# A finished head group's skip, gate and squares one tile per half unit, and the squares written over the gate

## The chip, the cores and the metric

The kernel runs on one core of a Trainium2 chip. A core has a matrix engine (TensorE, PE in the profile, with its weight loads as PEld), a vector engine (VectorE, DVE), a scalar engine (ScalarE, ACT), a general engine (GpSimd, POOL) and a queue engine that issues most DMAs (SyncE, SP). The metric is device time of one launch in microseconds.

## The reference

One step of a two-layer decoder over 512 prompt tokens and 8 x 4 sample tokens, 544 columns in all, of width 1024. Layer A is a Mamba-2 mixer: a projection to a gate `z` (2048), to `x|B|C` (3072) and to `dt`; a causal convolution of width 4 with SiLU on `x|B|C`; a chunked recurrence over 32 heads in 4 groups; then

```python
y, s_final = ssd_scan(xs * dt[..., None], dt * a, bm, cm, ssm_init.astype(jnp.float32))
y = y + xs * d_skip.astype(jnp.float32)[:, None]
y = rmsnorm(y.reshape(b, l, SSM_INNER) * jax.nn.silu(z.astype(jnp.float32)), g_gate)
return y.astype(h.dtype) @ w_out, new_conv, s_final
```

Three things of this are done for each finished head group, and the change is about them: the skip (`y + xs * d_skip`), the gate (times SiLU of `z`), and the squares that the norm needs. Layer B is a dilated window attention on a shared K/V; a last RMSNorm ends the step. Layer B, the K/V projection and the norms behind the layers are not touched.

## The kernel before

Features lie on the 128 partitions, tokens on the free axis, so one tile of a feature block is 128x544. A head group has 512 inner features, four such tiles, held together in one "slab" of 128x4x544. The pool `slab` has 13 of them; the halves of the normalized input (`xh`, `xl`, four slabs), `BT` and `CT`, the recurrence's output `v`, its input `xs`, the gate `uz` and later the split outputs `vh`, `vl` all come from it. A slab is free again when the last instruction that reads it is done.

Matrix products are done in three passes on a split of float32 into a high and a low part, 24 matmuls for one half of the tokens: `pa` for columns 0 to 255, `pb` for 256 to 543. Three PSUM banks (tag `pj`) serve all projections, five (tag `ss`) the recurrence.

*The units.* The recurrence is cut into 24 units, six per group: four chunks of 128 prompt tokens and, after the second and the fourth, two quads of four sample rows each (`ssm_chunk`, L602; `ssm_quad`, L663). Each unit is a generator with a first part (load, decay, transposes) and a second part (state update and output, written into `v`); a quad has a third, its last state update, whose store (L746, on ScalarE's DMA queue) frees the buffer for the next quad's load of states (L685, on SyncE's). A quad's states sit in two buffers.

*The filler.* Between these parts the loop draws steps from a filler, one matmul per step: the projections of `x|B|C` and `z`, tile by tile, in the order of `IN_ORDER` (L46 to L51). `PACE` (L55) says how many steps a unit gets: 57, 62, 64 and 44 for the four groups, half of them between the unit's own first part and the second part of the unit before, and half before that unit's third part. A tile of `x`, `B` or `C` ends in `conv`: ScalarE copies the two PSUM halves into `cb` (L331, L336, L337), makes the first product `co` (L527), VectorE adds three more (L529), ScalarE takes the tanh (L531), and VectorE writes the result (L532, L533). GpSimd writes the edges of `cb` (L329, L330) and saves the last rows (L523, L524). A tile of `z` ends in `z_part` (L562): a tanh into `zth`, then VectorE writes the gate into `uz`. A weight tile is split by ScalarE (L199) and VectorE (L200).

*The "t" buffers.* `cb`, `co`, `zth` and `sq` share one tag with four buffers of up to 571 columns:

```python
    def tt(name, cols=T):
        return wk.tile([128, cols], F32, name=name, tag="t", bufs=4)
```

*The finish of a group.* At units 6, 12, 18 and 24 the loop calls `gate_skip` for the group that has just ended. It issues four skips on VectorE (L584), and for every tile whose gate is done already `gate_mul_a`: the product with `uz` (L592; GpSimd, for the last group VectorE), the square on ScalarE into a "t" buffer `sq` (L597; the first of all goes straight into `ssq`, L594), and the sum into `ssq` on GpSimd (L598). Tiles whose gate comes later are multiplied at the end of their `z_tile`.

*What sets the order.* The program is written for a scheduler that puts each engine's instructions in order beforehand, by priority (the written order, but for parts marked as urgent) and by when it expects their inputs and buffers. On the chip every engine then keeps that order; a waiting instruction holds up what stands behind it on its engine.

Of the kernel before, what the change touches and what calls it, by code (L numbers as in the profile page):

```python
# [14 lines left out]
AF = mybir.ActivationFunctionType  # L15
ALU = mybir.AluOpType
# [108 lines left out]
def tile_yoco_step(  # L125
# [6 lines left out]
    nc = tc.nc  # L132
# [21 lines left out]
    def half(name, dt=F32, shape=(128, 4, T)):  # L154
        return slab.tile(list(shape), dt, name=name, tag="s")

    def pj(name, cols=512):
        return psum.tile([128, cols], F32, name=name, tag="pj", bufs=3)
# [61 lines left out]
    def proj_steps(p, ws, act_h, act_l, c0, c1, k0=0, k1=None, order=None):  # L220
        n = len(ws) * 8
        o = p[:, 0:c1 - c0]
        order = order or range(n)
        for i in range(k0, n if k1 is None else k1):
            k = order[i]
            hi, lo = ws[k // 8]
            ah, al = act_h[k // 4][:, k % 4, c0:c1], act_l[k // 4][:, k % 4, c0:c1]
            mm(o, hi[:, k % 8, :], ah, start=i == 0, stop=False)
            yield
            mm(o, hi[:, k % 8, :], al, start=False, stop=False)  # L230
            yield
            mm(o, lo[:, k % 8, :], ah, start=False, stop=i == n - 1)
            yield
# [63 lines left out]
    def tt(name, cols=T):  # L297
        return wk.tile([128, cols], F32, name=name, tag="t", bufs=4)
# [18 lines left out]
    dsk = ac.tile([128, 16], F32, name="dsk")  # L317
# [67 lines left out]
    for i in range(2):  # L385
        sq, xa = sqx[i][:, :, 0:HA], x_t[i][:, :, 0:HA]
# [157 lines left out]
    v_t = [None] * 4  # L544
    xs_t, uz_t = {}, {}
    v_done, z_done = set(), {}
    ssq = ac.tile([128, T], F32, name="ssq")
# [14 lines left out]
    def z_part(g, i, th, p, c0, c1):  # L562
        p = p[:, 0:c1 - c0]
        nc.scalar.activation(th[:, c0:c1], p, AF.Tanh, scale=0.5)
        nc.vector.scalar_tensor_tensor(uz_t[g][:, i, c0:c1], th[:, c0:c1], 1.0, p, op0=ALU.add, op1=ALU.mult)

    def z_tile(zi, w):
        g, i = zi // 4, zi % 4
        if i == 0:
            uz_t[g] = half("uz")  # L570
        th = tt("zth")
        for c0, c1 in ((0, HA), (HA, T)):
            p = pj("pa" if c0 == 0 else "pb")
            yield from proj_steps(p, [w], x_h, x_l, c0, c1)
            z_part(g, i, th, p, c0, c1)
        z_done[g] = i + 1
        if g in v_done:
            gate_mul_a(g, i)

    def gate_skip(g):  # L580
        v, xs = v_t[g], xs_t[g]
        for i in range(4):
            vi = v[:, i, :]
            nc.vector.scalar_tensor_tensor(vi, xs[:, i, :], dsk[:, 4 * g + i:4 * g + i + 1], vi, op0=ALU.mult, op1=ALU.add)  # L584
        v_done.add(g)
        for i in range(z_done.get(g, 0)):
            gate_mul_a(g, i)

    def gate_mul_a(g, i):
        vi, uz = v_t[g][:, i, :], uz_t[g][:, i, :]  # L590
        last = g == 3
        (nc.vector if last else nc.gpsimd).tensor_tensor(vi, vi, uz, op=ALU.mult)  # L592
        if g == 0 and i == 0:
            nc.scalar.activation(ssq, vi, AF.Square)  # L594
            return
        sq = tt("sq")
        nc.scalar.activation(sq, vi, AF.Square)  # L597
        nc.gpsimd.tensor_tensor(ssq, ssq, sq, op=ALU.add)  # L598

    grp = {}  # L600

# [163 lines left out]
    def filler_a():  # L765
        nxt = load_w(w_in[5])
        for i, (kind, t) in enumerate(IN_ORDER):
            if i < 5:
                continue
            w = nxt  # L770
            if i + 1 < len(IN_ORDER):
                nxt = load_w(w_in[i + 1])
            else:
                out_first.append(load_w(w_out[0, :, 0:8, :]))
            yield from (conv_tile if kind == "x" else z_tile)(t, w)
            if kind == "x" and t == 3:
                yield from tok_transposes()
            if kind == "z" and t in (13, 14):
                for j in range(4):
                    v_split(t - 13, j)  # L780

    def run(n):
        for _ in range(n):
            if next(fill, 0) == 0:
                return
# [22 lines left out]
    for u in range(len(units) + 1):  # L808
        pace = PACE[min(u, len(units) - 1) // 6]
        if u < len(units):  # L810
            live.append(units[u][0](*units[u][1]))
            next(live[u])
        run(pace // 2)
        if u:
            next(live[u - 1], 0)
            run(pace - pace // 2)
            next(live[u - 1], 0)
            if u == len(units):
                run(10000)
            if u % 6 == 0:  # L820
                gate_skip(u // 6 - 1)
        else:
            run(pace - pace // 2)
    run(10000)
# [711 lines left out]
    for u in range(len(units) + LA + 2):  # L1536
        i = u - LA
# [111 lines left out]
```

## Time and profile before

| | |
|---|---|
| median of 3 runs | 942.71 us (940.88 to 947.96) |
| the profiled execution | 942.13 us |
| its span | 940.4 us |
| TensorE busy / its mean granted clock | 917.3 us (98%) / 0.991 |
| VectorE, ScalarE, GpSimd busy | 682.7, 479.3 and 203.3 us |
| layer A's recurrence, from its first to its last unit | about 80 to 361 us of the span |
| skips of groups 0 to 3 | from 153.8, 230.1, 305.6 and 361.8 us |

All rows are of one profiled execution; times in them are in microseconds from the start of the span, durations in a group's row are means in nanoseconds. L592 means line 592 of the kernel before. In a list of waits, a row says who waited, for whom, for how long in total, how many times, and the longest. In the chain of waits, a row has its start, its length, and what ran or was waited for. In a table by stretches, a row has the stretch, its length, the busy time of PE, PEld, DVE, ACT and POOL with the number of instructions, then TensorE's granted clock as a share of full speed, the busy share of the DMA engines, and GB/s. In a row of an engine's order, the brackets hold the idle time before it and what ended that.

### The profile page before, as it was taken

What the parts mean: (1) busy time and instruction counts of PE and PEld (TensorE: products, weight loads), DVE (VectorE), ACT (ScalarE), POOL (GpSimd) and SP (SyncE); (2) the same over time, 40 slices, a digit from 0 to 9 for tenths busy, and PEclk for the clock granted to TensorE, in tenths of its full rate; (3) what the DMA queues carried; (4) which work ended last, traced back from release to release, by engine and by line L of the source; (5) the groups of instructions that cost most, each with busy time, mean ns of one, the idle gap of its engine ahead of it and who ended that gap; (6) DMA issues with size and microseconds to landing.
All of it is one profiled execution on the core that took longest, in us unless ns stands there. A gap on an engine that the chain in (4) does not pass through costs nothing.

```text
span 940.4 us, 21836 instructions
## 1 busy us (share of the span) xinstructions
PE 917.3 (98%) x8659; PEld 846.0 (90%) x8659; DVE 682.7 (73%) x1421; ACT 479.3 (51%) x1071; POOL 203.3 (22%) x297
## 2 busy tenths in 40 slices
PE   7999999899899999999999999999999999999996
PEld 5999888789798889999999999988888888888996
DVE  6688988997998889644489336876677766778632
ACT  5557754645555654422255213555555555557642
POOL 2232644723826642111101000000000000000021
PEclk9999999899999999999999999999999999999999
DMA  7252255264454543536277555757767767775411
GB/s 260 89 141 94 101 196 180 93 202 133 165 169 153 182 161 110 157 113 220 89 253 231 185 189 184 268 182 267 245 202 260 266 213 254 267 257 184 155 48 48
DMA packets 75951, 168.49 MB, mean 179 GB/s; under 512 B 19463, under 2 KB 37209, under 8 KB 75337
## 3 DMA queue, kind: packets, MB, share of 16 engines
q1 hardware_dynamic: 71608, 154.63, 50.2%
q10 hardware_dynamic: 3168, 9.72, 2.6%
q0 software_dynamic: 1072, 2.74, 1.1%
q8 instruction: 68, 1.11, 0.5%
q14 instruction: 35, 0.28, 0.1%
HBM read 141.14 MB, written 25.93 MB: 178 GB/s over the span
## 4 chain that ended last, share of the span: by engine, by line
PE 91%; DVE 4%; DMA 2%; ACT 1%; POOL 1%; issue 0%; DVEq 0%; ACTq 0%; SPq 0%
PE pa L143 36%; PE pb L143 31%; PE sp L143 3%; PE so L143 3%; PE pv L143 2%; PE s L143 2%; PE yd L143 2%; PE csp L143 1%; PE yo L143 1%; PE xp L146 1%; PE ptp L146 1%; PE w L146 1%; PE yos L143 1%; PE up L143 1%; POOL v L592 1%; DMA kc<-ck 1%
## 5 line engine op out<-in xcount | busy, mean ns | idle before, releaser
L199 ACT ACTIVATE whi<-wraw 128x1024 fp32r<-128x1024 f32 x72 | 76.1, 1057 | 95.8 <-PE pb L143 63.3
L200 DVE TENSOR_TENSOR wlo<-wraw,whi 128x1024 fp32r<-128x1024 f32 x71 | 89.2, 1256 | 47.0 <-ACT whi L199 46.6
L143 PE MATMUL pa<-bq,whi 128*128 128x272 f32 x512 | 103.1, 296 | 0.0
L143 PE MATMUL pa<-xh,whi 128*128 128x256 f32 (+1 forms) x320 | 93.1, 294 | 3.3 <-ACT xh L365 3.3
L143 PE MATMUL pb<-xh,whi 128*128 128x288 f32 (+1 forms) x304 | 91.0, 301 | 3.9 <-ACT cb L331 3.9
L143 PE MATMUL pb<-xl,whi 128*128 128x288 f32 (+1 forms) x304 | 91.8, 304 | 0.9 <-DVE xl L368 0.8
L143 PE MATMUL pa<-xl,whi 128*128 128x256 f32 (+1 forms) x320 | 90.8, 287 | 1.1 <-DVE xl L368 1.1
L143 PE MATMUL pb<-xh,wlo 128*128 128x288 f32 (+1 forms) x304 | 88.1, 301 | 0.0
L143 PE MATMUL pa<-xh,wlo 128*128 128x256 f32 (+1 forms) x320 | 85.0, 283 | 0.0
L143 PEld LDWEIGHTS pa<-bq,whi 128*128 128x128 f32 x512 | 81.3, 189 | 0.9
L143 PE MATMUL pb<-bq,whi 128*128 128x272 f32 x384 | 77.1, 295 | 0.5 <-DVE kv L1114 0.5
L143 PE MATMUL pa<-bq,wlo 128*128 128x272 f32 x256 | 74.2, 290 | 0.0
L529 DVE SCALAR_TENSOR_TENSOR co<-cb,cvp,co 128x568 f32<-128x568 f32 x72 | 66.3, 921 | 1.1
L143 PEld LDWEIGHTS pa<-xh,whi 128*128 128x128 f32 x320 | 60.9, 190 | 6.2 <-ACT xh L365 3.7
L143 PEld LDWEIGHTS pb<-xl,whi 128*128 128x128 f32 x304 | 58.3, 192 | 6.5 <-issue 4.4
L143 PEld LDWEIGHTS pa<-xl,whi 128*128 128x128 f32 x320 | 60.8, 190 | 3.5 <-DVE xl L368 1.6
L143 PEld LDWEIGHTS pb<-xh,whi 128*128 128x128 f32 x304 | 58.5, 192 | 5.0 <-ACT cb L331 4.1
L143 PEld LDWEIGHTS pb<-bq,whi 128*128 128x128 f32 x384 | 60.8, 189 | 1.6 <-DVE kv L1114 0.8
L1350 POOL COPY lse<-mxs 128x1 f32<-128x1 f32 x16 | 4.6, 287 | 266.9 <-DVE mxs L1348 266.9
L143 PEld LDWEIGHTS pa<-xh,wlo 128*128 128x128 f32 x320 | 58.1, 189 | 1.3 <-issue 0.9
L143 PEld LDWEIGHTS pb<-xh,wlo 128*128 128x128 f32 x304 | 57.2, 192 | 2.2 <-issue 2.2
L1173 ACT ACTIVATE whi<-wraw 128x512 fp32r<-128x512 f32 x64 | 40.1, 627 | 36.7 <-PE pa L143 17.0
(389 smaller groups left out, 2771.0 us busy)
## 6 DMA issues: line engine op xcount, KB each, us to landing
wraw<-w_in SPq DMA_DIRECT2D x40, 512.0 KB
kc<-ck SPq DMA_DIRECT2D x32, 640.0 KB
vc<-cv SPq DMA_DIRECT2D x32, 640.0 KB
wraw<-wb SPq DMA_DIRECT2D x32, 512.0 KB
s<-s SPq DMA_DIRECT2D x16, 512.0 KB
m<-aed SPq DMA_DIRECT2D x16, 512.0 KB
ssmS<-s ACTq DMA_DIRECT2D x16, 512.0 KB
wraw<-w_out SPq DMA_DIRECT2D x16, 512.0 KB
```

The source lines that it names most:

```text
L143: pin(nc.tensor.matmul(*a, **k))
L146: pin(nc.tensor.transpose(*a))
L199: a = nc.scalar.activation(hi, raw, AF.Copy)
L200: b = lo_eng.tensor_tensor(lo, raw, f32(hi), op=ALU.subtract)
L529: nc.vector.scalar_tensor_tensor(o, cb[:, k:k + n], cvp[:, ti, k:k + 1], o, op0=ALU.mult, op1=ALU.add)
L592: (nc.vector if last else nc.gpsimd).tensor_tensor(vi, vi, uz, op=ALU.mult)
L1173: nc.scalar.activation(hi, src[p][j], AF.Copy)
L1350: nc.gpsimd.tensor_copy(lse[:, i16:i16 + 1], mx[:, 2:3])
```

## The change

A finished group's four tiles go into a list `skips`. The loop takes one tile from it at the start of a unit and one in the middle, after the second part of the unit before, so a group's finish is spread over the next two units. The tile's product, square and sum follow its skip at once if its gate is done; otherwise they follow at the end of its `z_tile`, as before, for which the set `v_done` now holds pairs of group and tile. After the last unit the list is emptied before the rest of the filler, where before the filler ran to its end first. The square goes into the tile's own gate `uz`, which the product has just read, and no longer takes a "t" buffer.

```diff
-        if g in v_done:
+        if (g, i) in v_done:
             gate_mul_a(g, i)
 
-    def gate_skip(g):
-        v, xs = v_t[g], xs_t[g]
-        for i in range(4):
-            vi = v[:, i, :]
-            nc.vector.scalar_tensor_tensor(vi, xs[:, i, :], dsk[:, 4 * g + i:4 * g + i + 1], vi, op0=ALU.mult, op1=ALU.add)
-        v_done.add(g)
-        for i in range(z_done.get(g, 0)):
+    skips = []
+
+    def skip_one():
+        if not skips:
+            return
+        g, i = skips.pop(0)
+        vi = v_t[g][:, i, :]
+        nc.vector.scalar_tensor_tensor(vi, xs_t[g][:, i, :], dsk[:, 4 * g + i:4 * g + i + 1], vi, op0=ALU.mult, op1=ALU.add)
+        v_done.add((g, i))
+        if i < z_done.get(g, 0):
             gate_mul_a(g, i)
...
-        sq = tt("sq")
-        nc.scalar.activation(sq, vi, AF.Square)
-        nc.gpsimd.tensor_tensor(ssq, ssq, sq, op=ALU.add)
+        nc.scalar.activation(uz, vi, AF.Square)
+        nc.gpsimd.tensor_tensor(ssq, ssq, uz, op=ALU.add)
...
+        skip_one()
         run(pace // 2)
         if u:
             next(live[u - 1], 0)
+            skip_one()
             run(pace - pace // 2)
             next(live[u - 1], 0)
+            if u and u % 6 == 0:
+                skips += [(u // 6 - 1, i) for i in range(4)]
             if u == len(units):
+                while skips:
+                    skip_one()
                 run(10000)
-            if u % 6 == 0:
-                gate_skip(u // 6 - 1)
         else:
             run(pace - pace // 2)
```

## The prediction

> **What bounds the kernel now.** I read the page's busy times first, then the list of who waited for whom, for the matrix engine alone, from 40 to 420 us (the stage that the change touches), then the chain of waits and the order of the other engines around each wait found.
>
> ```profile
> PE 917.3 (98%) x8659; PEld 846.0 (90%) x8659; DVE 682.7 (73%) x1421; ACT 479.3 (51%) x1071; POOL 203.3 (22%) x297
> ```
> ```profile
> PE pb L143 <- ACT cb L331: 3.9, 1, 3.9
> PE yos L143 <- DMA s<-s: 2.5, 1, 2.5
> ```
>
> TensorE is the bound, and in the touched stage it waits just twice. So the change can win only what these two waits cost, and can lose wherever it makes a third. A table by stretches (us, busy PE, PEld, DVE, ACT, POOL, then the granted clock) gives each wait and what follows it:
>
> ```profile
> 163.83:167.77 3.94, 0.01 (x1) 0.00 (x1) 3.94 (x4) 1.56 (x4) 3.86 (x3) 0.80 0.89 356
> 167.77:173.00 5.23, 5.23 (x23) 5.17 (x23) 5.12 (x7) 3.05 (x9) 4.67 (x8) 0.50 0.00 0
> 244.02:246.55 2.53, 0.00 (x0) 0.00 (x1) 2.50 (x6) 0.64 (x2) 2.36 (x8) 1.00 0.92 303
> 248.00:252.00 4.00, 4.00 (x22) 4.00 (x21) 3.30 (x6) 4.00 (x10) 4.00 (x4) 0.57 0.13 52
> ```
>
> The first wait costs 3.94 us, and then 5.23 us run at clock 0.50, half of which is lost: 2.6. Together 6.5. The second costs 2.53 and then 4.00 x (1 - 0.57) = 1.7, together 4.2. The prize is 10.8 us (6.55 + 4.25 unrounded), no more. A practical rule of the Trainium skill (TensorE: Matmul & The Clock Gate, section Why this matters for your kernels) asks for no idle gaps above about 3 us between bursts; by it the second gap would lose no clock, and the prize would be 9.1. The 0.57 row speaks against it, and I go by the row.
>
> **The first wait: who holds it.** The chain of waits, then ScalarE's own order there:
>
> ```profile
> 161.46 1.80 DVE v L584
> 163.26 0.07 issue
> 163.33 2.24 POOL v L592
> 165.58 1.75 POOL ssq L598
> 167.32 0.02 issue
> 167.34 0.38 ACT cb L331
> 167.73 0.04 issue
> 167.77 0.61 PE pb L143
> ```
> ```profile
> 165.61 0.66 ACT L597 ACTIVATE sq<-v 128x544 f32<-128x544 f32 x1 [2.25 <-POOL v L592]
> 166.17 0.57 ACT L650 COPY st<-csp 128x512 f32<-128x512 f32 x1
> 167.34 0.37 ACT L331 COPY cb<-pa 128x256 f32<-128x256 f32 x1 [0.60 <-POOL ssq L598]
> ```
>
> This is group 0's finish: skip (L584), gate (L592), square (L597), sum (L598). TensorE's next projection needs a PSUM bank that the copy into `cb` frees. That copy lacks a buffer of the four tagged "t", because squares sit in them until GpSimd has summed them; and it also stands on ScalarE behind the last square, which had stood there 2.25 us for GpSimd's product. The change takes away both holds: the square goes over the gate `uz` and takes no "t" buffer, and the four pieces come one per half unit, so at most one or two of the four are still ahead of this copy. I count 6.5 us gained. What is late next is VectorE, below.
>
> **The second wait.** It is another part of the same finish, of group 1:
>
> ```profile
> 230.75 0.49 PE L143 MATMUL up<-xr,btr 32*128 32x512 f32 x1
> ```
> ```profile
> 230.13 5.08 DVE L584 SCALAR_TENSOR_TENSOR v<-xs,dsk,v 128x544 f32<-128x544 f32 x4
> 235.13 1.21 DVE L200 TENSOR_TENSOR wlo<-wraw,whi 128x1024 fp32r<-128x1024 f32 x1
> 236.26 0.80 DVE L529 SCALAR_TENSOR_TENSOR co<-cb,cvp,co 128x568 f32<-128x568 f32 x1
> 236.99 0.68 DVE L744 TENSOR_TENSOR s<-up,s 128x512 f32<-128x512 f32 x1
> ```
> ```profile
> 238.37 4.51 DMA ssmS<-s
> 242.89 0.02 SPq L685
> 242.91 0.03 issue
> 242.94 3.57 DMA s<-s
> 246.51 0.04 issue
> 246.55 1.05 PE yos L143 x4
> ```
>
> The last state update of quad 1 is ready on TensorE at 230.75 + 0.49 = 231.2, but VectorE adds it at 236.99, behind four skips in one piece (5.08). Its store then leaves at 238.37, the load into the same buffer at 242.94, and TensorE wants it at 244.02. With no skip ahead, the update can go about 5.1 us earlier. The store follows the update by 238.37 - 236.99 - 0.68 = 0.7 (ScalarE's queue, held by the same copy into `cb`), so it leaves near 233, and the load lands near 241.4 instead of 246.5, 2.6 us before it is wanted. I count 4.2 gained. Even if two skips stay ahead (half of 5.08), the 2.53 is just gone.
>
> **What the moved steps cost.** Per tile, one VectorE skip, one GpSimd product (VectorE for group 3), one ScalarE square, one GpSimd sum; no DMA. Their grouped rows:
>
> ```profile
> L584 DVE SCALAR_TENSOR_TENSOR v<-xs,dsk,v x16: 772/778/1884, 153.8 to 363.8; 128x544 f32<-128x544 f32 x16
> ```
> ```profile
> L598 POOL TENSOR_TENSOR ssq<-ssq,sq 128x544 f32<-128x544 f32 x15 | 23.7, 1581 | 28.4 <-ACT sq L597 28.0
> L592 POOL TENSOR_TENSOR v<-v,uz 128x544 f32<-128x544 f32 x12 | 21.6, 1805 | 31.1 <-DVE v L584 16.1 <-DVE uz L565 15.0
> ```
>
> Counts and shapes stay, so nothing is saved or added in work. A tile costs GpSimd 1.8 + 1.6 = 3.4 us, and there are four per boundary, 13.6. They move past the next group's first chunk and quad: on GpSimd past the state decays and the small copies into the next `cb`; on ScalarE a square waits for its product with the next copies behind it; on SyncE nothing moves. The square waits for the same product as before, so that wait is not new. Two slabs live longer: `xs` by about one and a half units, `uz` until the sum rather than the product. By my count of live slabs the pool of 13 is just full at groups 1 and 2 (four halves of x, BT and CT, three or four `v`, two `xs`, one or two `uz`) and not over, so I take zero; a first write delayed by one square and sum, 0.66 + 1.6 = 2.3 us, is the other end, beside TensorE's queued matmuls.
>
> The term that I can't read off is VectorE's slack. Its busy time (third) in the stretches after each finish:
>
> ```profile
> 150.00:206.00 56.00, 52.06 (x406) 46.52 (x405) 54.38 (x79) 31.16 (x65) 30.79 (x41) 0.94 0.43 145
> 206.00:230.00 24.00, 24.00 (x205) 21.61 (x204) 17.92 (x36) 13.23 (x32) 8.62 (x16) 1.00 0.48 158
> 230.00:280.00 50.00, 47.47 (x369) 41.73 (x369) 47.61 (x70) 29.38 (x62) 27.04 (x37) 0.97 0.48 160
> 280.00:361.00 81.00, 81.00 (x675) 71.03 (x675) 70.60 (x119) 45.39 (x97) 42.11 (x42) 1.00 0.48 165
> ```
>
> Without the first wait TensorE would pass the first stretch in 56.0 - 6.5 = 49.5 us, with 54.4 of VectorE work beside it: VectorE falls 4.9 us further behind. It has 24.0 - 17.9 = 6.1 us free in the next stretch to recover. In the third, 47.6 against 50.0 - 4.2 = 45.8 leaves 1.8. If the buffers bear no lag, 6.7 us of the prize come back; if they bear all, 0. VectorE ran 97% busy through the first stretch and TensorE waited only where squares held the buffers, so I am nearer to 0 and take 1.5.
>
> **Sum.** The profiled execution took 942.13 us (span 940.4 and 1.7 around it), 0.6 below the median of 942.71. 942.1 - 10.8 + 1.5 = 932.8; I say 933.
>
> **The rivals.**
> *One gap stays.* ScalarE's order is fixed beforehand; a square or a tanh that waits for a late VectorE result still holds the copy into `cb`. For it: 2.25 us of such waiting in the row of 165.61. Against: only one piece at a time now. With the first gap kept, 942.1 - 4.2 = 937.9; with the second kept, 942.1 - 6.5 = 935.6.
>
> *The order hardly moves.* The scheduler places instructions by priority and readiness, so the written place isn't the placed one:
>
> ```profile
> 158.88 0.77 DVE L584 SCALAR_TENSOR_TENSOR v<-xs,dsk,v 128x544 f32<-128x544 f32 x1
> 159.58 1.88 DVE L529 SCALAR_TENSOR_TENSOR co<-cb,cvp,co 128x568 f32<-128x568 f32 x1
> 161.39 1.87 DVE L584 SCALAR_TENSOR_TENSOR v<-xs,dsk,v 128x544 f32<-128x544 f32 x1
> ```
>
> Here skips written in one piece are already split by other work. Then just the freed buffers count: the copy into `cb` gains its 0.60 wait, the store about 0.7; 942.1 - 1.3 = 940.8.
>
> *Slower: VectorE becomes the bound.* A skip takes 0.77 alone and 1.87 beside GpSimd's product, 1.1 more; a convolution step at 159.58 shows the same. If the 8 GpSimd operations of a boundary, now strewn among convolution steps, each lengthened one such step more than before, VectorE would gain 8 x 1.1 = 8.8 us of work per boundary at the low end, and 8 x 1.8 = 14.4 if each blocked for a whole product. Group 0: lag 4.9 + 8.8 to 14.4, less the 6.1 of slack, is 7.6 to 13.2 us of waiting, with 2.6 of slow clock after it; group 1, lag 1.8 and the same additions, has 81.0 - 70.6 = 10.4 us of slack behind it, and gives 0 to 7.5 (5.8 and 1.7 of clock). Against the prize: 942.1 - 10.8 + 10.2 to 23.3, or 941.5 to 954.6, middle 948. It decides once the lag passes 6.1. Against it: the lengthened rows are in the 54.4 already. The Trainium skill (SBUF — State Buffer, section SBUF: two separate sides) calls the port pair that VectorE and GpSimd share an exclusive lock held for a whole instruction; by that rule the upper end, 954.6, would hold, while the 1.1 above, less than a whole product of 1.8, shows partial overlaps only.
>
> **Chances and range.** Both gaps go 0.52 (931 to 935); one stays 0.22 (935.6 or 937.9); order hardly moves 0.13 (940.8); slower 0.13 (about 948). The runs shown lie down to 940.88, 1.3 below the profiled one, so the low end is 931.3 - 1.3 = 930.0, less half a microsecond for the clock rows, which are means: 929.5; the high end is 943, past the third case; outside lie the slower case and little else. One per cent, about what a measurement of this kernel can tell from no change, is 9.4 us, or 933.3. My forecast lies on that line: some six tenths of its 0.52 are beyond it, 0.31, and a little of the second case, 0.32 in all. Slower by over 1% (952) is half of the last case, 0.07. The rest, 0.61, is within.
>
> **What will show it.** In the profile after: the list of TensorE's waits before 300 us has neither row; the granted clock holds 1.00 from 150 to 260; squares appear as `uz`; the skips stand singly, with the last state update of each quad 1 ahead of them; the store after group 1's last state update leaves within 3 us of the matmul that feeds it (231.2 to 238.4 now). A TensorE wait on VectorE or ScalarE at 165 to 215 would show the lag paid. Convolution steps of 1.9 us in greater number between 155 and 185 would show the slower case. Wrong altogether would be a gain above 11 us, or any change after 400 us.

## The result and the profile after

The changed kernel takes 948.69 us in the median of 20 runs (944.53 to 951.53), the kernel before 942.63 beside it. The ratio is 1.0054, 95% interval 1.0042 to 1.0067: 0.5% slower, about 5 us (the two medians lie 6.1 apart). The prediction was 933, with 943 as its upper end. The profiled execution took 946.2 us with a span of 944.4, 4.0 more than before. The first line of its page:

```profile
PE 920.4 (97%) x8659; PEld 848.3 (90%) x8659; DVE 682.0 (72%) x1421; ACT 479.1 (51%) x1071; POOL 201.4 (21%) x297
```

Counts are as before and busy times nearly so (TensorE 3.1 us more); TensorE is again busy nearly throughout. What changed is whom it waits for. The list of TensorE's waits from 40 to 420 us had two rows; now it has five:

```profile
PE pb L143 <- DVE uz L565: 2.8, 1, 2.8
PE xp L146 <- DVE xdd L715: 2.1, 1, 2.1
PE yos L143 <- DMA s<-s: 1.7, 1, 1.7
PE up L143 <- DVE xdd L629: 1.1, 2, 0.7
PE up L143 <- DVE cbm L631: 0.5, 1, 0.5
```

The row `pb <- ACT cb` is gone, so the first gap closed. The row for the load (`yos <- DMA s`) stayed, smaller. The other four rows are new, and all of them name VectorE. (Lines behind the diff are two or three higher than before: L587 is the skip, L595 the gate product, L599 the square, L600 the sum, L746 the state update.)

**The first gap: won, then handed back.** TensorE's own order (start, length, and in brackets the wait before it and its cause):

```profile
166.80 1.06 PE L143 MATMUL yos<-s,cp 128*32 128x512 f32 x8
181.30 0.74 PE L146 MATMUL xp<-ident,xs 128*128 128x128 f32 x4 [2.15 <-DVE xdd L715]
189.37 0.46 PE L143 MATMUL up<-xr,btr 32*128 32x512 f32 x1 [0.45 <-DVE xdd L629]
190.29 0.46 PE L143 MATMUL up<-xr,btr 32*128 32x512 f32 x1 [0.46 <-DVE cbm L631]
```

The quad's `yos` starts at 166.80; before it started at 173.18. That is 6.4 us, the whole prize of the first gap. But the next chunk's transposes need a PSUM bank that the quad's `xdd` must first have read, and VectorE comes to that late, behind a weight split and convolution steps that are longer beside GpSimd's work (2.06 us and 1.55 each, against 1.21 and 0.80 from 186.09 and 187.82, where GpSimd is idle):

```profile
175.56 2.06 DVE L200 TENSOR_TENSOR wlo<-wraw,whi 128x1024 fp32r<-128x1024 f32 x1
177.55 3.10 DVE L529 SCALAR_TENSOR_TENSOR co<-cb,cvp,co 128x568 f32<-128x568 f32 x2
180.57 0.68 DVE L715 TENSOR_TENSOR xdd<-xp,tok 128x512 f32<-128x512 f32 x1
```

Three short waits follow, and after them the clock falls. The table by stretches (us, busy PE, PEld, DVE, ACT, POOL, granted clock):

```profile
182.00:185.00 3.00, 3.00 (x16) 3.00 (x15) 3.00 (x5) 2.94 (x8) 2.35 (x8) 0.50 0.00 0
189.00:192.00 3.00, 2.18 (x12) 1.69 (x13) 3.00 (x6) 0.68 (x1) 0.00 (x0) 1.00 0.58 194
192.00:195.00 3.00, 3.00 (x16) 3.00 (x15) 3.00 (x10) 2.27 (x4) 0.52 (x4) 0.50 0.01 3
```

The waits are 2.15 + 0.45 + 0.46 = 3.1 us, the two stretches at half clock cost 1.5 each: 6.1 of the 7.3 by which the lead of 6.4 has become a lag of 0.9 at 196.

The late `xdd` has two possible causes: VectorE's load, and its place in VectorE's order. Its input `xp` was written by 166.9, and by the program one of the three buffers tagged `xd` came free, at the latest, with these matmuls:

```profile
173.51 1.09 PE L143 MATMUL yd<-m,xdt 128*64 128x128 f32 x16
```

So `xdd` could have gone at 174.6, but it stood behind the split and the two steps until 180.57. In the kernel before, `yd` ended at 181.0 and `xdd` went at 181.25, behind the same three steps. TensorE came 6 us earlier, and VectorE's order there stayed as it was.

**The second gap: hardly touched.** VectorE's order around group 1's finish, and the store on ScalarE's queue:

```profile
230.54 5.06 DVE L587 SCALAR_TENSOR_TENSOR v<-xs,dsk,v 128x544 f32<-128x544 f32 x4
237.38 0.68 DVE L746 TENSOR_TENSOR s<-up,s 128x512 f32<-128x512 f32 x1
238.09 0.34 ACTq L748 DMA_DIRECT2D ssmS<-s  x1
```

The four skips are written singly but still stand in one piece ahead of the last state update (230.13 with 5.08, 236.99 and 238.37 before). I take it that the scheduler placed the ready skips where it expected VectorE to be idle, in front of an update that must wait for TensorE; what shows is the order, not the reason. The load's wait fell from 2.53 to 1.65, and no slow clock follows it.

**The tail: a loss that I had not looked for.** VectorE's order in the last group's finish, and TensorE's wait there:

```profile
362.76 1.47 DVE L587 SCALAR_TENSOR_TENSOR v<-xs,dsk,v 128x544 f32<-128x544 f32 x2
364.15 1.35 DVE L595 TENSOR_TENSOR v<-v,uz 128x544 f32<-128x544 f32 x2
365.42 2.58 DVE L587 SCALAR_TENSOR_TENSOR v<-xs,dsk,v 128x544 f32<-128x544 f32 x2
367.93 2.35 DVE L200 TENSOR_TENSOR wlo<-wraw,whi 128x1024 fp32r<-128x1024 f32 x1
370.20 0.41 DVE L565 SCALAR_TENSOR_TENSOR uz<-zth,pa 128x256 f32<-128x256 f32 x1
```
```profile
370.66 0.40 PE L143 MATMUL pb<-xh,whi 128*128 128x288 f32 x1 [2.82 <-DVE uz L565]
```

In the changed kernel the last group's skips and products are written ahead of the rest of the filler. They now stand on VectorE ahead of a gate part (L565) that frees TensorE's projection bank; before, that gate part came first, at 361.43. The norm's first matmul starts at 385.28, against 380.87 before.

### The profile page after: what moved, and what is told of

The parts are those of the page before. It is cut to its first block, busy times and chain, and to the rows that moved or that the text cites. A ratio compares the mean times of both kernels' runs of the same rounds, so it can differ in the third digit from the quotient of the medians.

```text
span 944.4 us, 21836 instructions
## 1 busy us (share of the span) xinstructions
PE 920.4 (97%) x8659; PEld 848.3 (90%) x8659; DVE 682.0 (72%) x1421; ACT 479.1 (51%) x1071; POOL 201.4 (21%) x297
## 4 chain that ended last, share of the span: by engine, by line
PE 83%; DVE 8%; DMA 4%; ACT 2%; issue 1%; POOL 0%; DVEq 0%; SPq 0%; ACTq 0%
PE pa L143 34%; PE pb L143 28%; PE sp L143 3%; PE so L143 3%; DMA m<-aed 2%; PE pv L143 2%; PE s L143 2%; DVE wlo L200 1%; DVE co L529 1%; PE yd L143 1%; PE csp L143 1%; PE ptp L146 1%; PE w L146 1%; PE yo L143 1%; DVE v L587 1%
## 5 line engine op out<-in xcount | busy, mean ns | idle before, releaser
L200 DVE TENSOR_TENSOR wlo<-wraw,whi 128x1024 fp32r<-128x1024 f32 x71 | 91.9, 1294 | 51.4 <-ACT whi L199 51.2
```

Source lines behind the costliest of these rows:

```text
L200: b = lo_eng.tensor_tensor(lo, raw, f32(hi), op=ALU.subtract)
```

## The experiments

To compare kernels I read from each trace when TensorE starts a unit (its first transpose into `cbp`), and subtract the kernel before's time for the same unit. Units count from 0: unit 6 opens group 1, unit 10 stands behind the first gap and what follows it, unit 13 before the second gap, unit 15 behind it, unit 23 is the last quad. Up to unit 6 nothing differs by design, but the traces already lie between 0.3 us ahead and 2.7 behind at unit 0, and waits of 0.2 to 1.2 us between 121 and 136 us come and go. So the column "6 to 10" (the difference gained or lost between those units) is the one to read for the first gap. All in us, one profiled execution each; the ratio is to the kernel before.

| kernel | ratio, 95% interval | unit 6 | unit 10 | 6 to 10 | unit 13 | unit 15 | unit 19 | unit 23 |
|---|---|---|---|---|---|---|---|---|
| before, its own times | | 144.21 | 195.79 | 51.58 | 231.17 | 260.29 | 304.84 | 341.50 |
| the changed kernel | 1.0054, 1.0042 to 1.0067 | +0.2 | +0.9 | +0.7 | +0.9 | -1.6 | +1.3 | +1.3 |
| 1 only squares moved | 1.0012, 0.999 to 1.0033 | +1.3 | +1.3 | 0.0 | +1.3 | +0.2 | +1.1 | +1.1 |
| 2 only skips singly | 1.0049, 1.0032 to 1.0067 | +0.8 | +2.3 | +1.6 | +2.3 | -0.3 | +0.8 | +0.8 |
| 3 changed, old tail | 1.0003, 0.998 to 1.0026 | +1.8 | +2.5 | +0.7 | +2.5 | +0.7 | +0.6 | +0.6 |
| 4 as 3, skips held singly | 1.0059, 1.0033 to 1.0084 | +3.2 | +7.8 | +4.6 | +7.9 | +3.0 | +7.8 | +7.8 |
| 5 as 1, no skips in group 0 | 0.9976, 0.9961 to 0.9991 | +3.6 | +0.9 | -2.7 | +0.9 | -1.3 | +0.3 | +0.3 |
| 6 as 1, no GpSimd gate work in group 0 | 0.9942, 0.9925 to 0.996 | +1.1 | -4.9 | -6.0 | -4.9 | -7.2 | -6.2 | -6.2 |
| 7 as 1, group 0's finish 4 units later | 1.0017, 1.0002 to 1.0031 | +2.3 | -4.3 | -6.6 | +4.4 | +2.3 | +4.1 | +4.1 |
| 8 as 7, group 1's too | 1.0082, 1.0064 to 1.0101 | +3.5 | -3.1 | -6.6 | +6.4 | +1.3 | +9.9 | +10.1 |
| 9 as 1, products on VectorE | 1.0006, 0.999 to 1.0023 | +0.4 | +0.4 | 0.0 | +0.4 | -4.2 | +0.1 | +0.3 |
| 10 as 9, sums too | 1.0028, 1.001 to 1.0046 | -0.1 | -0.7 | -0.6 | -0.7 | -5.5 | -1.9 | +2.7 |
| 11 as 1, group 1's skips behind the update | 1.0017, 0.9999 to 1.0035 | +2.3 | +2.3 | 0.0 | +2.3 | -2.8 | +1.6 | +1.6 |
| 12 = 9 and 11 | 1.0012, 0.9992 to 1.0033 | +0.7 | +1.4 | +0.7 | +1.4 | -3.7 | +1.3 | +1.3 |
| 13 = 7 and 9 | 0.9987, 0.9965 to 1.0009 | +2.4 | -4.1 | -6.6 | +0.5 | -4.6 | 0.0 | +0.8 |
| 14 before, more VectorE work | 1.0052, 1.003 to 1.0074 | +2.3 | +6.8 | +4.5 | +7.3 | +7.2 | +7.1 | +7.1 |
| 15 = 13 and 11 | 1.0003, 0.9983 to 1.0024 | +1.8 | -4.8 | -6.6 | -0.3 | -5.4 | -2.4 | -1.3 |
| 16 as 13, finish singly | 0.9974, 0.9955 to 0.9993 | +3.1 | -3.4 | -6.6 | -2.4 | -7.5 | -5.1 | -3.6 |
| 17 = 16 and 11 | 0.9981, 0.9961 to 1.0001 | +1.8 | -4.8 | -6.6 | -3.8 | -8.8 | -4.1 | -4.1 |
| 18 as 16, half a unit earlier | 0.9996, 0.9977 to 1.0014 | +2.1 | -4.4 | -6.6 | +0.4 | -4.7 | -0.3 | +0.5 |

### The parts of the change

**1. Only the squares moved.** Skips in one piece and the tail as before.

```diff
-        sq = tt("sq")
-        nc.scalar.activation(sq, vi, AF.Square)
-        nc.gpsimd.tensor_tensor(ssq, ssq, sq, op=ALU.add)
+        nc.scalar.activation(uz, vi, AF.Square)
+        nc.gpsimd.tensor_tensor(ssq, ssq, uz, op=ALU.add)
```

> Only the squares are written over the gate; skips, sums and the tail stay in the old order. My theory (the buffers free TensorE at 164, VectorE is late right behind it and takes all of that back; the loss of the changed kernel comes from the tail's new order): the wait for cb at 164 is gone, waits on VectorE of some 3 us with half clock behind them appear between 180 and 198, the wait of 2.5 for the load after group 1 stays, the tail is as before, and the time is within 1.5 us of before (ratio 0.9985 to 1.0015). Rival A (it is the strewn skips and squares that slow VectorE, not the lag): with the skips in one piece the 6.4 us of the first gap are kept, about 936, ratio 0.993. Rival B (writing the square over the gate is itself what costs): a loss of 3 us or more, ratio above 1.003.

TensorE's waits in the stage, the three largest groups:

```profile
PE yos L143 <- DMA s<-s: 2.9, 1, 2.9
PE up L143 <- DVE xdd L626: 1.5, 2, 1.1
PE xp L146 <- ACT st L649: 1.2, 1, 1.2
```

As my theory had it, except that one of the new waits, at 168, is on ScalarE, and that those on VectorE between 180 and 198 come to 1.7 us, not some 3. The first gap is gone (unit 8 starts 6.0 us earlier, measured from unit 6), nothing of it is left at unit 10, and the time is that of before.

**2. Only the skips singly.** The changed kernel with the squares back in `tt("sq")`.

> Only the skips are written singly, with the changed kernel's order at the end; squares keep their buffers. My theory: the wait for cb at 164 stays about as it was (3 to 4 us and the half clock), so there is no lag behind it; the wait after group 1 stays about 2; the tail shows the wait of about 2.8 for uz and ends some 3 to 4 us later; ratio 1.003 to 1.005. Rival A (strewn work slows VectorE): waits on VectorE between 150 and 230 as in the changed kernel, on top of the gap, ratio 1.006 or more. Rival B (the squares' place is what costs): time as before, ratio 1.000.

Half wrong: the wait for `cb` is gone here too, although squares still take "t" buffers. Either half of the change closes the first gap by itself. Nothing of it is left at unit 10 either. The ratio lies where I expected it, which is luck: the gap that I left in went, and was lost again. The time is the changed kernel's, and the wait for `uz` in the tail is there: TensorE is 0.8 us behind at unit 23 and 5.4 at the norm's first matmul (386.28 against 380.87).

**3. The tail's old order back.**

```diff
             if u == len(units):
-                while skips:
-                    skip_one()
                 run(10000)
+                while skips:
+                    skip_one()
```

> The changed kernel with one difference: at the end of the recurrence the rest of the filler is written before the last group's skips, as it was before. My theory: the wait of 2.8 for uz at 371 goes, and the time comes back by 3 to 4.4 us, ratio to before 1.000 to 1.002. Rival A (strewn work between 150 and 310 is what costs): time as the changed kernel, ratio 1.004 to 1.006, since TensorE then waits elsewhere in the tail.

As expected: 0.6 us behind at unit 23, 0.7 at the norm's matmul, and the time of before. The written order at the end is what makes the changed kernel slower than before; the rest of the change comes out even, within the interval.

**4. The skips held singly.** As the third, with a hold on each skip of groups 0 to 2 that keeps VectorE to the written order.

```diff
-        nc.vector.scalar_tensor_tensor(vi, xs_t[g][:, i, :], dsk[:, 4 * g + i:4 * g + i + 1], vi, op0=ALU.mult, op1=ALU.add)
+        s = nc.vector.scalar_tensor_tensor(vi, xs_t[g][:, i, :], dsk[:, 4 * g + i:4 * g + i + 1], vi, op0=ALU.mult, op1=ALU.add)
+        if g < 3:
+            hold(s)
```

> The one before, and in addition the skips of groups 0 to 2 are held to the written order, so that they do stand singly and behind the last state update of the preceding group on VectorE. My theory: the store after group 1 leaves within 3 us of its matmul, the load lands before it is wanted and the wait of 1.65 near 245 is gone, worth 2 to 4 us of which VectorE's lag takes part back; ratio 0.996 to 1.000. Rival A (strewn skips beside GpSimd's work slow VectorE by more than they free): more waits on VectorE in 165 to 200 and 245 to 310 than in the run before it, ratio above 1.002. Rival C (the load after group 1 isn't ruled by the skips): the wait near 245 stays between 1.2 and 2.5.

Rival A's direction, but another mechanism. ScalarE's order, then VectorE's:

```profile
181.93 0.66 ACT L601 ACTIVATE uz<-v 128x544 f32<-128x544 f32 x1 [5.87 <-POOL v L597]
```
```profile
183.45 2.00 DVE L529 SCALAR_TENSOR_TENSOR co<-cb,cvp,co 128x568 f32<-128x568 f32 x2 [5.78 <-ACT co L527]
```

The third square stands on ScalarE 5.87 us for GpSimd's product, which itself stood on GpSimd behind four state decays (5.03 us from 175.55), although its skip was done at 175.3. Behind the square stands the product that a convolution starts with (L527), and VectorE idles 5.78 us for that. The finish of a tile runs through three engines; strewn out, each step can hold up the queue it stands in. It is the mechanism that the prediction named under "one gap stays", at another place. The wait for the load near 245 fell to 1.1, and TensorE gained 4.9 us between units 13 and 15, then lost them.

### What VectorE's lag is made of

**5. Without group 0's skips**, on top of the first kernel: the loop over the four skips is empty for group 0.

> The kernel with only the squares moved, and group 0's four skips left out (the product with D is missing from group 0's output; gate, squares and sums stay). That takes four VectorE steps, 3.1 to 5.1 us of its time, out of the stretch 150 to 206. My theory (VectorE's lag takes the first gap's gain back between 180 and 196): TensorE's waits on VectorE between 180 and 198 shrink, the third quad's neighbour at 196 comes 3 to 5 us earlier than in the run with the skips, and the time is 3 to 5 us under before, ratio 0.9945 to 0.997. Rival A (GpSimd's work beside VectorE is what costs, not VectorE's own steps): 0 to 1.5 us, ratio 0.998 to 1.001. Rival D (the place at 181 waits for the order of VectorE's queue or for a buffer, not for its load): no change there.

**6. Without group 0's gate work on GpSimd**, on top of the first kernel: `gate_mul_a` leaves group 0 without products, sums and three of its four squares (the first tile's goes into `ssq` as before).

> The same kernel with group 0's skips kept and its four GpSimd products with the gate, three squares and three GpSimd sums left out (group 0 is neither gated nor in the sum of squares, but for its first tile). That takes seven GpSimd steps away from beside VectorE. Rival A (port sharing is the cost): seven steps that each lengthen a VectorE step by 1.1 us, up to 7 us, time 3 to 7 us under before. My theory: most of the gain that VectorE's lag eats is its own work; 0 to 2.5 us under before, ratio 0.9975 to 1.000, less than the run without skips gains.

The fifth gained 2.7 us between units 6 and 10, the sixth 6.0: the reverse of what I expected. VectorE's own four steps are the smaller part; GpSimd's seven steps beside it are the larger. The stretch from unit 6 to unit 10, in the first, the fifth and the sixth kernel (third busy time: VectorE):

```profile
145.53:197.12 51.59, 47.91 (x378) 42.38 (x376) 49.75 (x72) 30.96 (x70) 31.20 (x38) 0.97 0.41 136
```
```profile
147.78:196.65 48.87, 47.47 (x379) 42.22 (x378) 45.33 (x68) 31.02 (x70) 28.78 (x38) 0.97 0.42 140
```
```profile
145.31:190.88 45.57, 45.46 (x378) 40.49 (x376) 41.08 (x70) 29.31 (x67) 15.27 (x31) 1.00 0.44 144
```

Without the skips VectorE is busy 4.4 us less, and the stretch is 2.7 shorter. Without GpSimd's work VectorE is busy 8.7 us less, although no step of its own was taken out. Two of the 72 steps, an update of 0.68 us and a convolution step of 0.80, fall just behind the end of that stretch, at 191.17 and 191.77; with them it is 7.2 less for the same steps. That is lengthening, 1.0 us for each of GpSimd's seven steps, close to the 1.1 of the prediction's row. The convolution's step, grouped over 150 to 198 us, shows it from the second row to the third: in the kernel before, in the first and in the sixth (count, busy us, mean ns). From the first row to the second GpSimd's work is the same, and part of the lengthening falls on other steps (the four skips' mean goes from 1050 to 1326 ns).

```profile
L529 DVE SCALAR_TENSOR_TENSOR co<-cb,cvp,co 128x568 f32<-128x568 f32 x13 | 15.3, 1180 | 0.1
```
```profile
L529 DVE SCALAR_TENSOR_TENSOR co<-cb,cvp,co 128x568 f32<-128x568 f32 x14 | 13.2, 941 | 0.1
```
```profile
L529 DVE SCALAR_TENSOR_TENSOR co<-cb,cvp,co 128x568 f32<-128x568 f32 x15 | 12.0, 801 | 0.1
```

The sixth kernel also leaves out three squares on ScalarE; how much of its 6.0 is theirs stays open.

**7 and 8. The finish four units later.** Group 0's skips, products and squares are written, and the skips held, at unit 10 instead of 6 (seventh); group 1's at unit 16 instead of 12 too (eighth; `AT` is then 10, 16, 18, 24).

```diff
+    AT = (10, 12, 18, 24)
...
-            if u % 6 == 0:
-                gate_skip(u // 6 - 1)
+            if u in AT:
+                gate_skip(AT.index(u))
```

> Nothing left out: the kernel with only the squares moved, and group 0's skips, gate and squares written four units later, where VectorE was 75% busy (206 to 230), and held there. My theory: VectorE is relieved in 150 to 206 by the same four steps and by the GpSimd products beside them, so the first gap's 6.4 us are kept for the larger part: TensorE at 196 is 3 to 6 us ahead of before, 0 to 2 of it lost again in 206 to 260 where the steps now lie; the wait for the load after group 1 stays or grows to 3 to 5; time 1 to 5 us under before, ratio 0.9945 to 0.999. Rival (what is moved only moves the waits, VectorE's whole load from 150 to 280 counts): within 1 us of before, ratio 0.999 to 1.001. Rival E (slabs: xs and the gate of group 0 are held longer and bring a new wait for a slab near 200 to 235): above 1.002.

> As the one before, and group 1's skips, gate and squares also four units later (from 231 to about 275), held there. My theory: the last state update of the quad before is no longer behind skips, the store leaves within 3 us of its matmul and the wait for the load near 245 goes, 2.5 to 4.2 us more than the run before it, less 0 to 2.5 for VectorE's load after 270; ratio 0.991 to 0.998. Rival C (the load is late for another reason): the wait near 245 stays at 1.5 to 2.9. Rival E (slabs): a new wait for a slab after 235, ratio above 1.000.

The first half of the expectation came out: TensorE wins 6.56 us between units 6 and 10, the whole prize of the first gap, and goes through that stretch without a wait. Then it loses 8.7 between units 10 and 13. In the seventh kernel ScalarE's order and TensorE's wait are

```profile
215.98 0.66 ACT L598 ACTIVATE uz<-v 128x544 f32<-128x544 f32 x1 [2.52 <-POOL v L594]
217.30 0.66 ACT L598 ACTIVATE uz<-v 128x544 f32<-128x544 f32 x1 [0.66 <-POOL v L594]
217.86 0.39 ACT L564 ACTIVATE zth<-pb 128x288 f32<-128x288 f32 x1
```
```profile
218.80 0.39 PE L143 MATMUL pa<-xh,whi 128*128 128x256 f32 x1 [1.16 <-DVE uz L565]
224.99 0.40 PE L143 MATMUL pb<-xh,whi 128*128 128x288 f32 x1 [3.07 <-DVE uz L565]
```

Squares that wait for GpSimd's product hold up the tanh (L564) of a gate tile, and with it the bank that TensorE needs. It isn't a slab (rival E). In the eighth the wait for the load after group 1 is gone, but group 1's finish makes new waits on VectorE between units 15 and 19, where TensorE loses 8.7 us.

### Where to put the work

**9 and 10. Products on VectorE; sums too.**

```diff
-        (nc.vector if last else nc.gpsimd).tensor_tensor(vi, vi, uz, op=ALU.mult)
+        nc.vector.tensor_tensor(vi, vi, uz, op=ALU.mult)
```

> The kernel with only the squares moved, and the products with the gate of groups 0 to 2 on VectorE in place of GpSimd. What is told apart: the run without skips gained 0.24% over before, the run without GpSimd's gate work 0.58%, so GpSimd's part looks dearer than VectorE's own steps. New theory (a GpSimd step beside VectorE lengthens VectorE's steps by about 1.1 us, and ScalarE's squares stand behind GpSimd's products): VectorE gets four steps of 0.7 a group and loses four lengthenings of 1.1, and the squares no longer hold ScalarE; the convolution step's mean in 150 to 198 falls from 0.94 to 0.80 to 0.88, TensorE at 196 is 2 to 5 us earlier, time 2 to 5 us under before, ratio 0.9945 to 0.998. Rival (VectorE's count of steps is what binds): 2.8 us more work a boundary, 2 to 6 us slower than before, ratio 1.002 to 1.006.

> As the one before, and the sums of squares on VectorE too, in all groups. New theory, port sharing alone: three more lengthenings of 1.1 go and three steps of 0.7 come for each group, 0 to 1.5 us better than the one before (ratio 0.993 to 0.998), unless the steps in the tail, where VectorE holds up the gate parts, cost it 1 to 3 us. Rival (VectorE's count of steps binds): 2 us a boundary slower than the one before, ratio above 1.002.

Neither side: 0.0 and -0.6 us between units 6 and 10. Four products on VectorE took 4.6 us there (1218 ns each), nearly what the lengthenings saved: VectorE's busy time over the stretch went from 49.75 to 48.20 us. In the ninth one wait of 3.2 us for `xdd` at 188 and the slow clock behind it take the gap's gain back. Here, moving the work between two engines that slow each other changed little. The tenth lost 4.6 more between units 19 and 23, where it waited 2.1 for a load at 315.

**11. Group 1's skips behind the last state update**, on top of the first kernel; nothing else moves.

```diff
+                if u == 12:
+                    with tc.issue_after(grp[1]["last"].ins):
+                        gate_skip(1)
```

> The kernel with only the squares moved, and group 1's skips put behind the quad's last state update on VectorE, nothing else changed. My theory of the second gap (the update stands behind four skips, so the store and the load that follows it are late): the store leaves within 3 us of its matmul, the wait of 2.9 for the load near 245 goes or falls under 0.5, and TensorE at 260 is 2 to 4 us earlier than in the run with only the squares moved; some of it is given back by 306, where VectorE is 87% busy, 0 to 2; ratio 0.996 to 0.999. Rival C (the load has another reason to be late): the wait stays above 1.5, ratio 0.999 to 1.002.

**12. The ninth and the eleventh together.**

> The squares moved, the products on VectorE, and group 1's skips behind the last state update. If the two mend different places the gains add: 4 to 8 us under before, ratio 0.9915 to 0.996. If TensorE's next wait on VectorE takes what either frees (as it did after the first gap): no better than the better of the two, within 1 us.

The eleventh shows the prediction's second cause, and that it wasn't worth anything alone. TensorE's last update matmul and the wait that came later, then the store:

```profile
233.08 0.49 PE L143 MATMUL up<-xr,btr 32*128 32x512 f32 x1
266.31 0.61 PE L143 MATMUL up<-xr,btr 32*128 32x512 f32 x2 [2.36 <-DVE xdd L626]
```
```profile
235.54 0.34 ACTq L745 DMA_DIRECT2D ssmS<-s  x1
```

The store leaves 2.0 us after its matmul ends (7.1 before), the wait for the load falls from 2.9 to 0.2, and TensorE gains 5.1 us between units 13 and 15 (the first kernel 1.1). At 266 it waits for VectorE, and by unit 16 4.5 of them are gone. The twelfth is no better than the ninth.

The next three ran as one set, in this order.

**13. The seventh and the ninth together**: group 0's finish at unit 10, products on VectorE.

> Nothing left out: group 0's finish four units later, as in the run that deferred it, and the gate products of groups 0 to 2 on VectorE, so that the squares on ScalarE no longer stand behind GpSimd. In the deferred run TensorE was 4.3 us ahead at 206 and lost 8.7 between 206 and 231, where ScalarE held tanh results behind squares that waited for GpSimd's products. Theory V (VectorE sets the pace in 144 to 197 and 231 to 306 and not in 206 to 230; what leaves the busy stretches is gained for good): TensorE stays 4 to 6 us ahead at 206, loses 0 to 2 by 231, and carries the rest to 306; ratio 0.994 to 0.998. Rival G (the load of the whole stretch 150 to 306 counts, wherever it stands): the lead is gone by 306, ratio 0.9995 to 1.002.

**14. The kernel before with more VectorE work.** One step that changes no value behind each of group 0's skips:

```diff
+            if g == 0:
+                nc.vector.scalar_tensor_tensor(xs[:, i, :], xs[:, i, :], 1.0, xs[:, i, :], op0=ALU.mult, op1=ALU.max)
```

> The kernel before, unchanged but for four more VectorE steps of 0.77 us (each multiplies one tile of group 0's x by 1.0 and takes the larger of it and itself, which changes no value), one behind each of group 0's skips: 3.1 us of VectorE's own work, up to 5 beside GpSimd, in the stretch 150 to 206. Theory V (VectorE sets the pace there even in the kernel before, and the wait for cb at 164 only showed it early): TensorE at 196 is 3 to 5 us later, ratio 1.003 to 1.006. By the accounting of the prediction (buffers bear VectorE's lag, which is made good in 206 to 230): at most 1 us, ratio 0.999 to 1.001.

**15. The thirteenth and the eleventh together.**

> The first kernel of this set, and group 1's skips behind the quad's last state update on VectorE. Theory V: in 231 to 306 VectorE sets the pace whatever TensorE waits for at 245, so the load is no longer waited for but TensorE at 306 is where it is without this, within 1 us; ratio within 0.001 of the first of this set. Rival (with the lead carried into this stretch the second gap is a gap of its own): 2 to 4 us better than the first of this set at 306.

The fourteenth is the plainest of all. Its only larger wait in the first stretch, and the stretch from unit 6 to 10:

```profile
PE pb L143 <- ACT cb L331: 7.5, 1, 7.5
```
```profile
146.55:202.58 56.03, 48.25 (x378) 42.89 (x376) 51.62 (x74) 31.05 (x70) 29.90 (x38) 0.91 0.34 116
```

VectorE is busy 51.62 us (74 steps) where before it was 48.42 (70 steps) for the same units; the stretch grew by 4.5, and the wait for `cb` from 3.9 to 7.5. So the kernel before already paid for VectorE's work there, at the place that the trace calls a wait for ScalarE. What this run does not tell apart is VectorE's load from the place of the skips: the added steps stand between them. The last skip goes at 169.45, 161.39 before, and on ScalarE the last square stands longer for its product, right ahead of the copy into `cb`:

```profile
169.45 1.84 DVE L584 SCALAR_TENSOR_TENSOR v<-xs,dsk,v 128x544 f32<-128x544 f32 x1
```
```profile
172.73 0.66 ACT L599 ACTIVATE sq<-v 128x544 f32<-128x544 f32 x1 [4.18 <-POOL v L594]
```

The thirteenth kept 4.1 us to unit 12 and lost 4.6 at 220, to a gate part that stood on VectorE behind four skips, three of them in one piece, and four products in one piece (a wait of 2.6, then slow clock). The fifteenth ended 2.4 us ahead at unit 19 and level with before in time.

**16 to 18. The deferred finish one tile per half unit.** Products on VectorE, group 0's tiles singly from unit 10 (sixteenth); the same with group 1's skips behind the update (seventeenth); from the second half of unit 9, `FIRST` 19 (eighteenth). The three ran as one set, in this order.

```diff
+    FIRST = 20
...
+        if 0 <= 2 * u - FIRST < 4:
+            gate_skip(0, [2 * u - FIRST])
         run(pace // 2)
...
+            if 0 <= 2 * u + 1 - FIRST < 4:
+                gate_skip(0, [2 * u + 1 - FIRST])
             run(pace - pace // 2)
```

> Nothing left out: squares moved, gate products on VectorE, and group 0's finish done one tile per half unit in units 10 and 11 (about 196 to 220), each skip held there. In the run that did the finish in one piece at unit 10 the 6.6 us won between 144 and 216 were lost for 4.6 at 220, where a gate part stood on VectorE behind four skips and four products. Theory V (VectorE has room in 206 to 230 if the finish doesn't stand in one piece ahead of what TensorE waits for): the wait for uz at 220 is under 1 us, TensorE at 231 is 4 to 6 us ahead of where it was at 144 relative to before, and stays so to 260; half or more of it is there at 306; ratio 0.993 to 0.998. Rival G (VectorE's load of the whole stretch counts): the lead at 306 is under 1 us, ratio 0.9985 to 1.001.

> As the one before, and group 1's skips behind the quad's last state update on VectorE. If the second gap is a gap of its own once VectorE is relieved: 2 to 4 us better at 306 than the one before it, ratio 0.990 to 0.996. If VectorE sets the pace in 231 to 306 in any case: within 1 us of the one before it.

> As the first of this set, but half a unit earlier (from the second half of unit 9, about 190), so the first tile's skip and product fall into the stretch where VectorE was 97% busy. Theory V: 1 to 2 us of the lead are lost at 196 to 207 against the first of this set; ratio 0.001 to 0.002 above it. Rival G: no difference.

The sixteenth's waits in the whole stage, and its stretch from unit 6 to 10:

```profile
PE up L143 <- DVE xdd L628: 1.7, 2, 1.2
PE yos L143 <- DMA s<-s: 1.0, 2, 0.5
PE xp L146 <- DVE v L737: 0.3, 1, 0.3
```
```profile
147.35:192.36 45.01, 45.01 (x378) 40.31 (x376) 39.41 (x67) 28.88 (x66) 16.59 (x31) 1.00 0.46 148
```

No wait for `cb`, no wait for `uz`, and clock 1.00 through the stretch, with 39.4 us of VectorE work in 45.0. It takes 941.23 us against 943.56 of before in the same comparison, ratio 0.9974, interval 0.9955 to 0.9993: 0.3% faster than the kernel before, and so faster than the changed one. The interval only just leaves out 1, and this is the best of all the kernels that leave nothing out, so the gain in time is weaker evidence than the stretch. From unit 6 to 19 it wins 8.2 us, of which 1.5 go again by unit 23. The seventeenth gains no more (0.9981). The eighteenth moved the first piece half a unit forward and lost 4.8 between units 11 and 12, at a place that I had not named:

```profile
192.26 0.78 DVE L584 SCALAR_TENSOR_TENSOR v<-xs,dsk,v 128x544 f32<-128x544 f32 x1
195.03 0.68 DVE L745 TENSOR_TENSOR s<-up,s 128x512 f32<-128x512 f32 x1
```
```profile
207.17 1.93 PE L143 MATMUL yos<-s,cp 128*32 128x512 f32 x8 [3.29 <-issue]
```

The skip stands ahead of the quad's last state update, which goes at 195.03 against 193.11 in the sixteenth; store and load follow by as much, and the next quad's `yos` starts after a wait of 3.29 that the trace gives no releaser for. By place and time it is the second gap's mechanism; that it is the load is argued from the order, not shown.

## Why the prediction was wrong

**Where the prize lies: right.** The two gaps cost what was worked out. Every kernel that took enough work out of the first stretch won 6.0 to 6.6 us there, against 6.5; the eleventh won 5.1 at the second, against 4.2.

**The first gap's cause: right, but too narrow.** It closes with the squares alone or with the skips singly alone. The fourteenth shows that VectorE's queue in that stretch sizes it too: 3.2 us more of its work made the same wait 3.6 us longer.

**The give-back: the step that failed.** The prediction saw that VectorE would have 54.4 us of work in 49.5, gave 0 to 6.7 as what might come back, and took 1.5, on the grounds that TensorE waited only where squares held the buffers and that VectorE could recover between 206 and 230. Measured between units 6 and 10, the changed kernel is 0.7 us behind before: the 6.5 of the first gap came back and 0.7 more, 7.2 within 30 us, above the top of that range. The lag never reached the slack at 206: as the row of 181.30 shows, the next unit's transposes wait for a bank that VectorE's late `xdd` has to empty. From unit 6 to unit 23, where the sum had a gain of 9.3 (10.8 less 1.5), the changed kernel lost 1.2.

That VectorE's work in the stretch is what takes the gain back is shown by the kernels that took work out (the fifth and the sixth) or moved it later (the seventh, the eighth and the five that build on them won 6.6 us each between units 6 and 10). Whether the same load in another order would do is open: no run moves `xdd` ahead of the split and the convolution steps.

**The second gap's cause: right; that the change removes it: wrong.** This is the rival "the order hardly moves", for group 1: the skips stayed in one piece ahead of the update. The prediction gave that 0.13 and priced it at -1.3. The store left 238.09 - 231.60 - 0.49 = 6.0 us after its matmul, not within 3. Measured, TensorE gained 2.4 us from unit 14 to 15 and lost 2.7 from unit 18 to 19, again for VectorE.

**The slower rival: right in its result by luck, wrong in its mechanism.** VectorE did become what TensorE waits for, and 948 was its middle. But that price holds nothing for the tail, and it asked for additional lengthening by strewn GpSimd work. VectorE's time from unit 6 to 10 rose only from 48.42 to 50.22 us, with two more steps inside the stretch (70 and 72), and the convolution's mean step in 150 to 198 went from 1180 to 1125 ns. No addition was needed: the work that was there sufficed, and it decided at once, not past a lag of 6.1.

**The tail: not seen.** The diff moves the last group's skips ahead of the rest of the filler, and the section on the change says so, yet the prediction names no cost for it and no term of the sum stood for it. It cost 3.1 us from unit 23 to the norm's first matmul, and with the old order back the changed kernel takes the time of before. This is the larger part of the loss. Beyond the norm nothing changed, as the prediction said (4.4 behind there, 4.0 at the end).

## What to carry to other kernels

When the bound engine's wait is taken away, ask what second engine runs beside that wait, and how full it is: here, at 97% busy, the wait was that engine's lag showing at its first place, and it showed again at the next. What helped here was to move such work out of the stretch, singly and to where the second engine had room; its steps have to be followed through every queue that they pass. And of a diff, every line that changes a written order needs its own term, also at the end of a loop.

## What the runs showed of the hardware

**Half clock for 3 us followed some short waits.** In the changed kernel 2.15 us of waiting at 181 is followed by 3 us at clock 0.50, and so are two waits of 0.45 and 0.46 at 189 to 190. The Trainium skill (TensorE: Matmul & The Clock Gate, section Why this matters for your kernels) asks for no gaps above about 3 us; here the clock fell behind shorter ones. But it isn't length alone: behind the wait of 1.65 at 245 and behind that of 2.82 at 370 the clock stayed at 1.00.

```profile
247.00:250.00 3.00, 3.00 (x23) 2.50 (x20) 2.96 (x7) 1.83 (x5) 3.00 (x4) 1.00 0.47 179
372.00:375.00 3.00, 3.00 (x25) 3.00 (x25) 3.00 (x3) 2.83 (x4) 1.78 (x1) 1.00 0.34 122
```

What decides, I can't say from these runs. A short wait here cost some 1.5 us of clock on top, or nothing; that is as much as many of the waits themselves.

**Seven GpSimd steps cost VectorE some 7 us.** In the first kernel the four products and three sums of group 0 were 7.9 + 4.9 = 12.8 us of GpSimd's time; with them gone VectorE was busy 7.2 us less for the same 72 steps, 56% of that. The Trainium skill (SBUF — State Buffer, section SBUF: two separate sides) has the port pair that the two share locked for a whole instruction; the share measured is below that, but it is more than the prize of the first gap, and the prediction had counted it as paid already.
